# An encoder's opening: zero products ahead of x, sums turned by transposes, later mask additions, new priorities, residual products last

## The chip, the cores and the metric

The kernel runs on one core of one Trainium2 chip. The metric is the device time of one execution in microseconds (us); lower is better. An execution's time is its span, from the first to the last instruction, and about 2 us around it.

## The reference, cut to what matters

Two layers of an encoder trunk work on x, 256 tokens of 1024 channels in float32. Each layer has a mixer and a feed-forward part, both conditioned by a vector c:

```python
mod = silu(c) @ ada_w + ada_b                     # six vectors of 1024
sh_m, sc_m, g_m, sh_f, sc_f, g_f = split(mod, 6)
h = rms_norm(x, norm_mix_g) * (1 + sc_m) + sh_m
proj = h @ w_in                                   # 1024 -> 5024 columns
(qa, ka, va, cq, ckv, kr, qc, kc, vc, ga, gb, gc) = split(proj)
o_na  = neighborhood_attention(qa, ka, va, na_rpb)
q_b   = rms_norm(cq, g) @ mla_w_uq;  kv_b = rms_norm(ckv, g) @ mla_w_ukv
o_mla = attention(...);  o_gqa = attention(...)   # merged by sigmoid gates, then w_out
x = x + g_m * (merged @ w_out)
h = rms_norm(x, norm_ffn_g) * (1 + sc_f) + sh_f
x = x + g_f * ((silu(gate) * up) @ ffn_w_down)    # gate, up = split(h @ ffn_w_gate_up)
```

After the second layer there is a last rms_norm. Matrix products are wanted in float32 accuracy.

## The kernel before, in words

**Products in three parts.** Each operand of a large product is split into a rounded part and the residual that the rounding leaves (`split_to`: a copy by ScalarE, a subtraction by VectorE). A product is then hi·whi + hi·wlo + lo·whi, lines L268, L269 and L270. Weights go through TensorE's moving side, 512 columns at a time, activations (`hi`, `lo`, 128x128) through the stationary side. The weights are cut into 248 items of up to 256 rows by 512 columns, 124 a layer. `load_split` fetches an item (SyncE issues the DMA, L247) and splits it into `whi` (ScalarE, L187) and `wlo` (VectorE, L188). There are five buffers for raw weights and seven for split ones. Each item is used twice, for the token halves t = 0 and t = 1. From item 12 on the second use stands four items behind the first.

**Order.** A list scheduler orders each engine's instructions: of those that are ready by its own model of the time, it takes the one with the smallest priority number, which is the place in the program unless `tc.high_priority()` moves it ahead. The queues that it writes are then worked off in order by each engine, whatever the chip's own times are. Within `tc.manual_schedule(engines={PE})` TensorE keeps the order of the program. `later(k, f)` puts a piece of work k uses of items behind; `at(i, f)` puts one ahead of item i.

**Opening.** x is loaded, squared and summed (`sumsq`, L192), scaled (L202), and turned by 16 transposes (`transposed`, L209), which ScalarE copies out (L834). The first layer's shift and scale (2 of the 6 vectors) are made a quarter (256 channels) at a time. `first_loads(q)` fetches 2 MB of `ada_w` in eight DMAs of 256 KB (L846). `first_sums(q)` forms eight products of 512 columns with `scz`, c's columns padded with zeros to 32, in four column groups of the array (L861); ScalarE copies the bank out as `four` (L864). In `four` the partial sums stand on rows 0, 32, 64 and 96. `first_mod(q)` adds them by four products of `four` with a column of ones (L870), makes A and B (L874 to L877), and modulates two of the eight channel blocks into `hi` and `lo` (L882 to L887). Items 0 to 11 are ordered so that the three items of a round need only the blocks of quarter q = 0, 1, 2, 3. `first_sums(q)` stands ahead of items 1, 4 and 7 (q = 1, 2, 3), `first_mod(q)` ahead of items 2, 5 and 8. Items 12 to 15 are the columns of qc. Item 16 (`mla_w_uq`) and item 17 (`mla_w_ukv`) take `cT` as their activations, item 18 begins the gates.

**cT.** `post_g1` copies cq, ckv and kr out of the bank (L363), squares them (L366), adds EPS (L370), takes the power -0.5 on GpSimd (L108), and scales (L374, L376). Nine uses later its second half `b_` transposes the result (L383), splits it into the two parts of `cT` (`split_to`, out `s`, in `tp`) and turns kr (L391 to L395).

**Masks.** `na_bias` fetches the relative position bias (two DMAs for each t, L345) and adds the window's mask to it, four VectorE additions for each t (L349). The first user is the softmax of the neighbourhood attention (L568), whose scores (L560) are formed ahead of item 18. In the first layer `na_bias` stands ahead of item 12. A softmax's result `P` goes to TensorE for transposes (L608).

## Time and profile before

| | |
|---|---|
| Median of 3 runs | 822.37 us (821.83 to 822.97) |
| The profiled execution: its own time | 822.51 us |
| Its span | 820.4 us |
| TensorE busy with matmuls | 790.7 us, 96% of the span |
| VectorE busy | 598.8 us, 73% |
| ScalarE busy | 453.7 us, 55% |
| Mean granted TensorE clock | 0.991 of full speed |
| DMA | 187.20 MB, mean 228 GB/s |

A row of a timeline gives the start, the length, the engine, the line in the kernel, the operation, what it writes and reads, and in brackets how long the engine was idle before it and what ended that idle time. PE is TensorE's matmul side, PEld its weight load, DVE VectorE, ACT ScalarE, POOL GpSimd, SPq SyncE's DMA queue. Busy times of matmuls overlap, so the start of the next matmul says more than the end of one.

### The profile page before, as it was taken

The page shows a single profiled execution, that of the slowest core. Times are in us where ns is not written, and L with a number is a line of the kernel's source. Part 1 is how long each engine was busy: PE and PEld are TensorE (multiplying, and loading weights), DVE is VectorE, ACT ScalarE, POOL GpSimd, SP SyncE. Part 2 cuts the span into 40 slices and gives each one's busy share as a digit, 9 for nine tenths or more (in the row PEclk, how much of TensorE's full clock was granted, in tenths as well). Part 3 has the DMA queues.
Part 4 walks back from the last instruction along what each step waited for, and adds up shares of the span by engine and source line. Part 5 has one row for each costly group of instructions (what it writes and reads, how often), then busy time and mean ns, then how long its engine had stood idle before and what let it go on. Part 6 is the DMA issues. An engine that isn't in the chain of part 4 may idle for free.

```text
span 820.4 us, 10803 instructions
## 1 busy us (share of the span) xinstructions
PE 790.7 (96%) x3776; PEld 633.4 (77%) x3776; DVE 598.8 (73%) x955; ACT 453.7 (55%) x788; POOL 25.8 (3%) x40
## 2 busy tenths in 40 slices
PE   5998999999999999999999999999999999999996
PEld 3786776788878888888878877777887888888884
DVE  3369898789777888875667699878978666665462
ACT  4365887644485444443466687774448544444441
POOL 1002100000000000000000020000000000000000
PEclk9999999999999999999999999999999999999998
DMA  9979488697667989886874668778765677876631
GB/s 315 359 245 273 131 293 252 198 311 227 194 180 241 322 294 306 276 264 190 210 213 137 180 192 279 222 230 283 250 198 182 219 233 223 259 226 184 182 103 52
DMA packets 113414, 187.20 MB, mean 228 GB/s; under 512 B 14672, under 2 KB 34256, under 8 KB 113360
## 3 DMA queue, kind: packets, MB, share of 16 engines
q1 hardware_dynamic: 113360, 186.51, 73.1%
q8 instruction: 30, 0.49, 0.3%
q14 instruction: 24, 0.20, 0.1%
HBM read 185.44 MB, written 1.05 MB: 227 GB/s over the span
## 4 chain that ended last, share of the span: by engine, by line
issue 49%; PE 31%; DVE 8%; DMA 6%; ACT 4%; POOL 1%; POOLq 0%; DVEq 0%; ACTq 0%
PE mm L268 8%; PE mm L270 8%; PE mm L269 8%; DMA raw<-in_ada_w_dram 6%; DVE wlo L188 2%; DVE acc L140 2%; PE tp L861 1%; POOL sm L108 1%; PE o L629 1%; ACT P L587 1%; ACT tm L218 1%; DVE sm L574 1%; PE tp L209 1%; PE tp L608 1%; PE tp L560 1%
## 5 line engine op out<-in xcount | busy, mean ns | idle before, releaser
L188 DVE TENSOR_TENSOR wlo<-raw,whi 128x1024 fp32r<-128x1024 f32 (+2 forms) x248 | 298.3, 1209 | 115.0 <-ACT whi L187 114.8
L187 ACT CAST whi<-raw 128x1024 fp32r<-128x1024 f32 (+2 forms) x248 | 256.9, 1041 | 221.6 <-PE mm L270 137.1
L268 PE MATMUL mm<-whi,hi 128*128 128x512 f32 (+1 forms) x784 | 314.0, 400 | 1.8 <-ACT hi L882 1.1
L270 PE MATMUL mm<-whi,lo 128*128 128x512 f32 (+1 forms) x784 | 307.1, 392 | 0.2
L269 PE MATMUL mm<-wlo,hi 128*128 128x512 f32 (+1 forms) x784 | 306.1, 390 | 0.5 <-DVE wlo L188 0.4
L268 PEld LDWEIGHTS mm<-whi,hi 128*128 128x128 f32 x784 | 148.1, 189 | 34.7 <-issue 5.7
L270 PEld LDWEIGHTS mm<-whi,lo 128*128 128x128 f32 x784 | 147.7, 188 | 32.8 <-DVE lo L188 1.8
L269 PEld LDWEIGHTS mm<-wlo,hi 128*128 128x128 f32 x784 | 148.3, 189 | 28.9 <-DVE wlo L188 1.7
L140 DVE SCALAR_TENSOR_TENSOR acc<-raw,sc,acc 128x512 f32<-128x512 f32 x140 | 104.9, 749 | 32.2 <-DMA raw<-in_ada_w_dram 30.5
L270 PE MATMUL mm<-whi,s 128*128 128x512 f32 (+1 forms) x188 | 73.3, 390 | 2.4 <-DVE s L188 2.4
L268 PE MATMUL mm<-whi,s 128*128 128x512 f32 (+1 forms) x188 | 74.2, 395 | 0.4 <-ACT s L187 0.4
L269 PE MATMUL mm<-wlo,s 128*128 128x512 f32 (+1 forms) x188 | 73.1, 389 | 0.0
L270 PEld LDWEIGHTS mm<-whi,s 128*128 128x128 f32 x188 | 35.4, 189 | 9.8 <-DVE s L188 2.6
L268 PEld LDWEIGHTS mm<-whi,s 128*128 128x128 f32 x188 | 35.3, 188 | 7.9 <-ACT s L187 0.9
L269 PEld LDWEIGHTS mm<-wlo,s 128*128 128x128 f32 x188 | 35.4, 188 | 6.8
L592 ACT ACTIVATE P<-P,sm 128x256 f32<-128x256 f32 x64 | 29.3, 509 | 5.7 <-DVE sm L590 5.6
L587 ACT ACTIVATE P<-tp,sm,rq 128x256 f32<-128x256 f32 x32 | 17.8, 561 | 15.9 <-DVE sm L584 15.8
L197 POOL TENSOR_SCALAR sm<-ss 128x1 f32<-128x1 f32 x10 | 4.0, 404 | 662.4 <-ACT tm L192 662.4
L218 ACT ACTIVATE tm<-tp,cm,cm 128x128 f32<-128x128 f32 x48 | 21.3, 472 | 6.2 <-PE tp L209 6.2
L108 POOL TENSOR_TENSOR sm<-sm,nhalf 128x1 f32<-128x1 f32 (+2 forms) x22 | 18.4, 835 | 127.1 <-DVE sm L370 65.2
L192 ACT ACTIVATE tm<-x_sb 128x512 f32<-128x512 f32 x20 | 12.6, 632 | 16.8 <-DVE x_sb L703 14.6
L733 DVE TENSOR_TENSOR tm<-tm,mm 128x512 f32<-128x512 f32 (+1 forms) x24 | 15.4, 640 | 8.7 <-PE mm L270 7.1
(157 smaller groups left out, 637.7 us busy)
## 6 DMA issues: line engine op xcount, KB each, us to landing
raw<-in_ada_w_dram SPq DMA_DIRECT2D x80, 512.0 KB, 4.8
raw<-in_w_gu_dram SPq DMA_DIRECT2D x80, 512.0 KB, 4.6
raw<-in_w_in_dram SPq DMA_DIRECT2D x64, 512.0 KB, 4.6
raw<-in_w_dn_dram SPq DMA_DIRECT2D x44, 512.0 KB, 4.8
s<-in_ada_w_dram SPq DMA_DIRECT2D x32, 256.0 KB, 6.7
raw<-in_w_out_dram SPq DMA_DIRECT2D x16, 512.0 KB, 4.9
raw<-in_w_in_dram SPq DMA_DIRECT2D x16, 256.0 KB, 5.0
raw<-in_w_gqa_dram SPq DMA_DIRECT2D x8, 512.0 KB, 5.6
```

The lines of the kernel that those rows point to most:

```text
L108: nc.gpsimd.tensor_tensor(out=r, in0=ms, in1=nhalf[:, 0:n], op=ALU.pow)
L140: nc.vector.scalar_tensor_tensor(out=acc, in0=raw[:, j, :], scalar=sc[:, kc:kc + 1], in1=acc, op0=ALU.mult, op1=ALU.add)
L187: nc.scalar.copy(hi_ap, src)
L188: nc.vector.tensor_tensor(out=lo_ap, in0=src, in1=hi_ap.bitcast(F32), op=ALU.subtract)
L192: nc.scalar.activation(junk, x_sb[:, t, hf * 512:(hf + 1) * 512], AF.Square, scale=1.0 / 32.0, accum_out=ss[:, hf:hf + 1])
L218: nc.scalar.activation(fv[:, j, :], xT[:, j, :], AF.Identity, scale=A[:, kc:kc + 1], bias=B[:, kc:kc + 1])
L268: nc.tensor.matmul(ps[t][:, 0:n], lhs(t, 0, kc), hi[:, j, 0:n], start=first, stop=False)
L269: nc.tensor.matmul(ps[t][:, 0:n], lhs(t, 0, kc), lo[:, j, 0:n], start=False, stop=False)
L270: nc.tensor.matmul(ps[t][:, 0:n], lhs(t, 1, kc), hi[:, j, 0:n], start=False, stop=last)
L587: nc.scalar.activation(pt[:, t, :], src[:, t, :], AF.Exp, bias=nb[:, t:t + 1], scale=scale[t], accum_out=rs[:, t:t + 1])
L592: nc.scalar.activation(pt[:, t, :], pt[:, t, :], AF.Copy, scale=rc[:, t:t + 1])
L733: nc.vector.tensor_tensor(out=hd[:, 0:n], in0=sgv, in1=up, op=ALU.mult)
```

## The change

Six edits are made together.

1. Sixteen products of 128x512 zeros (`warm`) stand on TensorE ahead of x's transposes, one more after `first_sums(0)` and one after `first_mod(0)`; their sums are read by nothing. The opening up to there is put in program order on TensorE.
2. `first_mod` no longer multiplies `four` with ones: it transposes its four blocks, and VectorE adds the four columns 0, 32, 64, 96 of each (`tensor_reduce`).
3. What follows in `first_mod` is a function of its own, `first_apply`, with high priority.
4. The mask additions become `na_mask`, five items behind the DMAs in the first layer (ahead of item 17), at the same place in the second.
5. `post_g1`'s chain from EPS to the scaled vectors, and the split of `cT`, get high priority.
6. Within an item the order over its two row blocks becomes hi·whi, hi·whi, hi·wlo, hi·wlo, lo·whi, lo·whi.

`tc.issue_after(last_pe())` only keeps TensorE's part of items 0 to 11 behind what was traced before it.

```diff
--- before.py
+++ after.py
@@ -91,6 +91,8 @@
 
     ones = cpool.tile([P, 1], F32, name="ones")
     nc.vector.memset(ones, 1.0)
+    zero1 = cpool.tile([P, 1], F32, name="zero1")
+    nc.vector.memset(zero1, 0.0)
     ones1 = cpool.tile([P, 2], F32R, name="ones1")
     nc.vector.tensor_copy(ones1, ones.to_broadcast([P, 2]))
     onesr = ones1[:, 0:1].to_broadcast([P, P])
@@ -262,12 +264,12 @@
                 if u == 0:
                     ps[t] = bank(t) if bank else psmm.tile([P, 512], F32, tag="mm", name=nm("mm"))
                 hi, lo = it["w"]
-                for j in range(nk):
-                    kc = 2 * u + j
-                    first, last = kc == 0, kc == nkc - 1
-                    nc.tensor.matmul(ps[t][:, 0:n], lhs(t, 0, kc), hi[:, j, 0:n], start=first, stop=False)
-                    nc.tensor.matmul(ps[t][:, 0:n], lhs(t, 0, kc), lo[:, j, 0:n], start=False, stop=False)
-                    nc.tensor.matmul(ps[t][:, 0:n], lhs(t, 1, kc), hi[:, j, 0:n], start=False, stop=last)
+
+                for n_, (part, w) in enumerate(((0, hi), (0, lo), (1, hi))):
+                    for j in range(nk):
+                        kc = 2 * u + j
+                        nc.tensor.matmul(ps[t][:, 0:n], lhs(t, part, kc), w[:, j, 0:n], start=(kc == 0 and n_ == 0),
+                                         stop=(kc == nkc - 1 and n_ == 2))
 
             pf = None
             if u == nu - 1:
@@ -337,13 +339,18 @@
 
         def na_bias():
             st["bias"] = []
+            st["hk"] = []
             for t in range(NT):
                 hk = t4([P, 16, W])
                 for r in range(2):
                     base = rpb[l, 2 * t + r]
                     src = bass.AP(tensor=base.tensor, offset=base.offset, ap=[[1, W], [127, 16], [1, W]])
                     nc.sync.dma_start(hk[r * W:(r + 1) * W], src)
-                b = t4([P, 16, W])
+                st["hk"].append(hk)
+
+        def na_mask():
+            for t in range(NT):
+                hk, b = st["hk"][t], t4([P, 16, W])
                 rev = bass.AP(tensor=hk.tensor, offset=hk.offset + W - 1, ap=[list(hk.ap[0]), [W, 16], [-1, W]])
                 for h in range(4):
                     nc.vector.tensor_tensor(out=b[:, 4 * h:4 * h + 4, :], in0=rev[:, 4 * h:4 * h + 4, :],
@@ -367,14 +374,15 @@
             nc.scalar.activation(junk[:, 256:384], c[:, 256:384], AF.Square, scale=float(128.0 ** -0.5),
                                  accum_out=s[:, 1:2])
             ms = sm(2)
-            nc.vector.tensor_scalar_add(ms, s, EPS)
-            r = rstd_of(ms, 2)
             rw = st["rw"]
             cn = t2([P, 384])
-            nc.vector.scalar_tensor_tensor(out=cn[:, 0:256], in0=c[:, 0:256], scalar=r[:, 0:1], in1=rw[:, 0:256],
-                                           op0=ALU.mult, op1=ALU.mult)
-            nc.vector.scalar_tensor_tensor(out=cn[:, 256:384], in0=c[:, 256:384], scalar=r[:, 1:2], in1=rw[:, 256:384],
-                                           op0=ALU.mult, op1=ALU.mult)
+            with tc.high_priority():
+                nc.vector.tensor_scalar_add(ms, s, EPS)
+                r = rstd_of(ms, 2)
+                nc.vector.scalar_tensor_tensor(out=cn[:, 0:256], in0=c[:, 0:256], scalar=r[:, 0:1], in1=rw[:, 0:256],
+                                               op0=ALU.mult, op1=ALU.mult)
+                nc.vector.scalar_tensor_tensor(out=cn[:, 256:384], in0=c[:, 256:384], scalar=r[:, 1:2],
+                                               in1=rw[:, 256:384], op0=ALU.mult, op1=ALU.mult)
 
             def b_():
                 tpt = tpb()
@@ -383,7 +391,8 @@
                     nc.tensor.transpose(tv[:, j, :], cn[:, j * P:(j + 1) * P], ident)
                 cT = t4([P, 2, 3, P], F32R)
                 st.setdefault("cT", {})[t] = cT
-                split_to(cT[:, 0], cT[:, 1], tv[:, 0:3, :])
+                with tc.high_priority():
+                    split_to(cT[:, 0], cT[:, 1], tv[:, 0:3, :])
                 kr = c[:, 384:416]
                 kpe = st["kpe"][:, t, :]
                 ab = t2([P, 2, 32])
@@ -651,6 +660,7 @@
         flush.add(i0)
         at(i0 + (7 if l == 0 else 0), params)
         at(i0 + (12 if l == 0 else 8), na_bias)
+        at(i0 + (17 if l == 0 else 8), na_mask)
 
 
         st["m"] = {}
@@ -822,6 +832,18 @@
         layer(l)
     xT0 = {}
 
+    warm_w = ppl.tile([P, 512], F32R, tag="pp", name="warm_w")
+    nc.vector.tensor_copy(warm_w, zero1.to_broadcast([P, 512]))
+    warm_ps = pso.tile([P, 512], F32, tag="o", name="warm_ps")
+
+    def warm(n):
+
+        for _ in range(n):
+            nc.tensor.matmul(warm_ps, warm_w[:, 0:P], warm_w, start=True, stop=True)
+
+    def last_pe():
+        return next(i for i in reversed(nc.cur_bb.bb.instructions) if i.engine == mybir.EngineType.PE)
+
     def first_x():
         xT = act.tile([P, KC, S], F32, tag="lo", name=nm("xT"))
         for hf in range(2):
@@ -865,9 +887,15 @@
         return four
 
     def first_mod(q, four):
-        red = tpb()
+        pv = tpb().rearrange("p (j q) -> p j q", j=4)
         for j in range(4):
-            nc.tensor.matmul(red[:, j:j + 1], four[:, j * P:(j + 1) * P], ones, start=True, stop=True)
+            nc.tensor.transpose(pv[:, j, :], four[:, j * P:(j + 1) * P], ident)
+        red = sm(4)
+        nc.vector.tensor_reduce(out=red, in_=pv.rearrange("p j (r z) -> p j r z", z=32)[:, :, :, 0], op=ALU.add, axis=AX.X)
+        with tc.high_priority():
+            first_apply(q, red)
+
+    def first_apply(q, red):
         k0 = 2 * q
         A, B, hT = mods[(0, 1)], mods[(0, 0)], state[0]["hT"]
         r2 = sm(2)
@@ -905,8 +933,13 @@
                 step(1, pend.pop(0))
         if i == 0:
             raws = first_loads(0)
-            first_x()
-            first_mod(0, first_sums(0, raws))
+            with tc.manual_schedule(engines={mybir.EngineType.PE}):
+                warm(16)
+                first_x()
+                four = first_sums(0, raws)
+                warm(1)
+                first_mod(0, four)
+                warm(1)
         for f in side.get(i, ()):
             f()
         load_split(it)
@@ -915,7 +948,7 @@
             q1 = i // 3 + 1
             if i % 3 == 1 and q1 < 4:
                 raws = first_loads(q1)
-            with tc.manual_schedule(engines={mybir.EngineType.PE}):
+            with tc.issue_after(last_pe()), tc.manual_schedule(engines={mybir.EngineType.PE}):
                 if i % 3 == 1 and q1 < 4:
                     four = first_sums(q1, raws)
                 if i % 3 == 2 and q1 < 4:
```

## Rows read from the trace of the kernel before

**Rows 1.** Windows: busy us and count by engine, granted clock, DMA share.

```profile
core 0: us, PE busy (x) PEld busy (x) DVE busy (x) ACT busy (x) POOL busy (x), PEclk, DMA share, GB/s
...
13.40:16.80 3.40, 2.21 (x16) 1.14 (x12) 0.35 (x3) 1.37 (x2) 0.00 (x0) 1.00 1.07 368
16.80:20.20 3.40, 2.34 (x6) 1.83 (x7) 3.35 (x6) 2.03 (x3) 0.00 (x0) 0.50 1.10 349
...
78.20:81.60 3.40, 3.40 (x13) 2.50 (x11) 3.40 (x9) 1.39 (x4) 0.00 (x0) 0.51 0.52 131
...
125.00:800.00 675.00, 667.00 (x3162) 540.58 (x3161) 509.39 (x754) 372.07 (x623) 13.79 (x20) 1.00 0.73 226
```

**Rows 2.** Timeline of the opening, TensorE.

```profile
7.82 3.68 PE L209 MATMUL tp<-con,tm 128*128 128x128 f32 x16 [7.82 <-DVE tm L202]
...
15.30 1.05 PE L870 MATMUL tp<-ones,tm 128*128 128x1 f32 x8 [0.73 <-ACT tm L864]
...
17.49 0.72 PE L268 MATMUL mm<-whi,hi 128*128 128x416 f32 x1 [1.14 <-ACT hi L882]
...
24.98 0.50 PE L268 MATMUL mm<-whi,hi 128*128 128x512 f32 x1
...
25.55 0.39 PE L270 MATMUL mm<-whi,lo 128*128 128x512 f32 x1
...
25.78 0.40 PE L268 MATMUL mm<-whi,hi 128*128 128x512 f32 x1
...
26.01 0.39 PE L269 MATMUL mm<-wlo,hi 128*128 128x512 f32 x1
...
33.84 1.92 PE L861 MATMUL tp<-s,scz 128*32 128x512 f32 x16
35.69 0.50 PE L268 MATMUL mm<-whi,hi 128*128 128x512 f32 x1
...
46.41 0.50 PE L268 MATMUL mm<-whi,hi 128*128 128x512 f32 x1
```

**Rows 3.** Quarter q = 1, last DMA: issue, then KB and us to landing.

```profile
15.82 0.37 SPq L846 DMA_DIRECT2D s<-in_ada_w_dram  x1
...
s<-in_ada_w_dram SPq DMA_DIRECT2D x1, 256.0 KB, 6.0
```

**Rows 4.** The same for q = 3.

```profile
38.25 0.37 SPq L846 DMA_DIRECT2D s<-in_ada_w_dram  x1
...
s<-in_ada_w_dram SPq DMA_DIRECT2D x1, 256.0 KB, 5.5
```

**Rows 5.** Timeline of TensorE around item 16.

```profile
66.42 0.49 PE L383 MATMUL tp<-con,tm 128*128 128x128 f32 x3
...
73.23 0.44 PE L268 MATMUL mm<-whi,s 128*128 128x384 f32 x1 [0.44 <-ACT s L187]
...
74.11 0.66 PE L407 MATMUL tp<-con,tm 128*128 128x128 f32 x4 [0.25 <-ACT s L408]
77.14 0.44 PE L270 MATMUL mm<-whi,s 128*128 128x384 f32 x1 [2.38 <-DVE s L188]
```

**Rows 6.** Timelines of ScalarE and VectorE around item 16.

```profile
72.72 0.85 ACT L187 CAST s<-tp 128x384 fp32r<-128x384 f32 x2
...
75.20 1.42 DVE L349 TENSOR_TENSOR s<-s,con 128x256 f32<-128x256 f32 x4
76.54 1.01 DVE L188 TENSOR_TENSOR s<-tp,s 128x384 fp32r<-128x384 f32 x2
...
82.82 0.42 DVE L568 SCALAR_TENSOR_TENSOR P<-tp,s 128x256 f32<-128x256 f32 x1 [0.55 <-PE tp L560]
```

**Rows 7.** Windows of VectorE to item 23; timeline row of its wlo.

```profile
62.50:97.10 34.60, 33.42 (x90) 0.95 0.73 193
97.10:102.50 5.40, 2.79 (x7) 1.00 0.69 237
...
101.24 1.22 DVE L188 TENSOR_TENSOR wlo<-raw,whi 128x1024 fp32r<-128x1024 f32 x1
```

## Prediction

> **What bounds the kernel now.** I read the windows first. From 125 to 800 us TensorE is busy 667 of 675 us at the full clock [rows 1], so behind the opening the kernel is as long as TensorE's work, and what is saved ahead of that reaches the end unless a later wait takes it back. Then I looked for the places ahead of 125 us where TensorE is idle or granted half its clock (1.2 GHz, not 2.4). There are two.
>
> The first is the opening. Item 0 starts at 17.49 us [rows 2]. Behind the stretch 13.4 to 16.8, in which TensorE was busy 2.21 of 3.40 us, half the clock is granted [rows 1], and item 0 runs at that. But the DMA engines are full there (share 1.07 and 1.10) [rows 1]. Item 1 stands behind `first_sums(1)`, which needs a quarter's eight DMAs. The last of them is issued at 15.82 and lands 6.0 us later, at 21.8 [rows 3]; for q = 3 it is 38.25 and 5.5, so 43.75 [rows 4]. Items 1 and 7 start at 24.98 and 46.41 [rows 2]. The reader is to see how little lies between: 3.2 and 2.7 us.
>
> The second is item 16. TensorE waits 0.44 us for `cT`'s rounded part, 0.25 for a bank that ScalarE empties, and 2.38 for `cT`'s residual part [rows 5]. That subtraction stands on VectorE right behind four mask additions, which end at 76.6 [rows 6]; the idle stretch is followed by half the clock from 78.2 to 81.6 [rows 1].
>
> **The change part by part.** *Zero products.* At the full clock 512-column products start 0.23 us apart (25.55, 25.78, 26.01) [rows 2]; at half the clock an estimate is twice that. Sixteen cost 3.7 to 7.4 us. Their operands need a memset and one copy on VectorE, which feeds L209 only at 7.82 [rows 2], so an estimate is that they start at 2 us and end between 5.7 and 9.4. The transposes begin at 7.82 [rows 2], so they may be held 1.6 us. That costs nothing: the sums behind them end with a landing, not with TensorE. If it went the other way and the clock is full, the 16 transposes need half of 3.68 us [rows 2], and this too ends at the landing. The two single products lie in TensorE's waits of 0.73 and 1.14 us [rows 2].
>
> What the clock can give is therefore bounded by the landings. `first_sums` comes in four steps, 1.85 us in all (33.84 to 35.69) [rows 2]; two of them, 0.9 us, may lie behind the last landing. Item 1 can then start at 21.8 + 0.9 = 22.7 instead of 24.98, 2.3 us earlier. Item 7 can start at 43.75 + 0.9 = 44.65 instead of 46.41 [rows 2], 1.75 us earlier. As the DMAs ran full before and are not changed, the later landing counts: **−1.75**. The lower end: TensorE stays at half the clock, and item 1 is won only by the 0.4 of the new sums and the 0.46 of the order within item 0 (both below), 0.9 in all.
>
> *Transposes for sums.* Eight steps by ones take 1.05 us (L870) [rows 2]; four transposes take 0.66 (L407) [rows 5]. The added reduction is a small VectorE operation; from the rows I have it lies between nothing and the 0.42 us of an operation on 256 columns [rows 6]. So 0.4 us less against 0 to 0.4 more in a chain whose end the landings set: 0. For q = 1 to 3 TensorE saves 0.4 us each, which the landings take too, but for the last: within the range.
>
> *Residual products last.* The number of products and weight loads stays. Before, L269 follows L268 with the same stationary block; afterwards no neighbours share one. From L270 to L268, which need different blocks, it is 0.23 us, from L268 to L269, which share one, 0.23 as well [rows 2]: sharing brought nothing that the rows show, so losing it costs 0, and at most what two decimals hide. For lateness the edit moves the first need of `wlo` by one product (0.23 us) and of a residual by two (0.46): at item 16 it would shorten the one long wait by 0.46, which the next edit removes whole. I take 0.
>
> *Masks and priorities.* The split of `cT` moves ahead of what ScalarE and VectorE did first. Its last transposes begin at 66.42 [rows 5], six us before ScalarE gets to it at 72.72, without an idle time ahead [rows 6]: its place in the queue made it late. With priority it is early, and the waits of 0.44, 0.25 and 2.38 go: **−3.0**. Without the idle stretch the clock stays, and what ran from 78.2 to 81.6 at half the clock [rows 1] takes half as long: **−1.7**. The mask additions, eight in 2.8 us (four take 1.42 [rows 6]), are still due ahead of L568, and VectorE was idle for only 0.55 us there, waiting for the scores [rows 6].
>
> *Given back.* TensorE would be 1.75 + 3.0 + 1.7 = 6.45 us ahead. Its next need that VectorE sets is `wlo` of item 23, made from 101.24 to 102.5 [rows 7]; counted in items, that is when TensorE takes item 23 up. From 62.5 to 97.1 VectorE is busy 33.42 of 34.60 us and then 2.79 of 5.40 [rows 7]: 3.8 us idle. Its inputs come 1.75 us earlier. If it closes all its idle time, it is 5.55 us ahead, and 0.9 us is given back; if none, 4.7. Much of that idle time is waiting for work that TensorE sends, and the end with it closed is the nearer one; I take **+1.8**.
>
> The profiled execution took 822.51 us, its span of 820.4 and 2.1 around it, which nothing here touches. The sum is −1.75 −3.0 −1.7 +1.8 = −4.65, so 817.86 for it; the median of the runs, 822.37, lies 0.14 lower, which makes **817.7 us** of the forecast. The cases below are worked from 822.4.
>
> **Rivals.** *Nothing is given back but 0.9*, or less because the scheduler orders VectorE anew (work with time in hand, as `wlo` of items 19 to 22, moves behind the softmax): 822.4 − 6.45 + 0.4 = 816.3. For it speaks that VectorE's order was written for a late TensorE.
>
> *VectorE's backlog takes it all:* the 4.7 us come back at the softmax and item 23, and only the opening's 1.75 is left: 820.7. For it speaks VectorE's 33.42 of 34.60 us.
>
> *The clock falls in the opening as before.* Ahead of item 0 TensorE has transposes, sums that wait for landings, and single products, which is not more than the 2.21 of 3.40 us after which half the clock was granted [rows 1]. Item 0 then runs at half the clock, as it did; the start of item 1 is won only by 0.9, and one of the two rounds behind it adds the 0.4 of its new sums before the landings stop it: 1.3 instead of 1.75, so 818.2. The Trainium skill speaks for this rival ("TensorE: Matmul & The Clock Gate", Part 4: PE-mode transpose): it says that transposes do not count as work for the clock gate, and both the turned x and the new sums are transposes. The trace neither agrees nor disagrees: transposes stood ahead of the full clock of 13.4, but sums stood between.
>
> *The other side: the neighbourhood softmax becomes late, twice.* If VectorE does the masks and the `wlo` of later items ahead of L568, its first softmax can start no later than its work then allows, 82.82 − 1.75 = 81.1, while the scores are there 6.45 us earlier than before, at 76.4. TensorE stands at L608 until the result comes, up to 4.7 us; an idle stretch of 2.4 us was enough to lose the clock (1.7 more). Once gives 822.4 − 6.45 + 6.4 = 822.4, no change. It decides when the second pair of heads, whose softmax stands behind the first in the same queue, loses the clock a second time: 824.1. Against it: VectorE never has more to do than before.
>
> **How the numbers follow.** The forecast's own case has 0.5 (816.8 to 819.5), little given back 0.17, the clock's case 0.1, the backlog 0.16, the late softmax 0.07. Below 0.2% (1.65 us), which is about what a measurement of this kernel tells from no change, "faster" ends at 820.7: the first three cases and half the backlog, 0.85. "Same" has the other half of the backlog and some of the late softmax, 0.1; "slower" 0.05. The range leaves out the late softmax and the outer ends of the others: 815.2 to 820.9.
>
> **What would show it.** Item 1's first product (L268, 512 columns) near 22.7 and item 7's near 44.6, both right behind a landing; no wait of L270 for `s` near 72 us, with `cT`'s casts on ScalarE close behind L383; full clock from about 24 us on; the waits that are left near L568, L608 and item 23. The prediction is wrong if the landings themselves come earlier or later, if `cT`'s cast stays behind the casts of weights, or if the list scheduler, whose choices downstream I cannot read from this trace, moves a wait into the steady part.

## The result and the profile after

Four runs of the changed kernel gave a median of 816.57 us (816.25 to 816.87), four of the kernel before beside them 822.67 (821.83 to 824.28): a ratio of 0.9917 [0.9897, 0.9938], faster by more than the 0.2% from which the prediction counts a change. The forecast was 817.7, its range 815.2 to 820.9. The profiled execution took 816.62 us, its span 814.7. Of the terms of the forecast some were too large and some too small, and one gain was put down to the wrong edit; the experiments show which.

Three windows of the changed kernel, their columns as in [rows 1]; the last is that of item 0:

```profile
78.20:81.60 3.40, 3.40 (x19) 2.44 (x19) 2.42 (x4) 2.89 (x7) 0.00 (x0) 1.00 0.27 84
125.00:800.00 675.00, 666.65 (x3162) 541.35 (x3161) 506.00 (x749) 368.73 (x615) 13.79 (x20) 1.00 0.70 225
...
17.00:20.40 3.40, 2.52 (x10) 1.80 (x11) 3.34 (x6) 2.03 (x3) 0.00 (x0) 1.00 1.10 348
```

Look at the granted clock, the third number from the end: 1.00 in every one, where in the kernel before two stretches had half of it. TensorE's work behind 125 us is what it was (666.65 us against 667.00), so nearly all of the gain was made ahead of that.

TensorE's timeline of the opening, to lay beside [rows 2]:

```profile
1.44 5.32 PE L842 MATMUL warm_ps<-warm_w 128*128 128x512 f32 x16 [1.44 <-DVE warm_w L836]
...
20.98 2.51 PE L883 MATMUL tp<-s,scz 128*32 128x512 f32 x16
23.42 0.73 PE L271 MATMUL mm<-whi,hi 128*128 128x512 f32 x2
...
26.28 0.60 PE L892 MATMUL tp<-con,tm 128*128 128x128 f32 x4
26.64 0.70 PE L271 MATMUL o<-whi,hi 128*128 128x512 f32 x2
...
30.59 0.79 PE L271 MATMUL mm<-whi,lo 128*128 128x416 f32 x2 [0.21 <-DVE lo L915]
...
34.29 0.73 PE L271 MATMUL mm<-whi,hi 128*128 128x512 f32 x2
...
43.30 1.92 PE L883 MATMUL tp<-s,scz 128*32 128x512 f32 x16
45.16 0.73 PE L271 MATMUL mm<-whi,hi 128*128 128x512 f32 x2
```

Item 1 starts at 23.42 instead of 24.98, item 4 at 34.29 instead of 35.69, item 7 at 45.16 instead of 46.41. The first is bound by a landing, the last isn't. The last DMAs of q = 1 and q = 3, first when SyncE issues them, then KB and the time to landing, against [rows 3, 4]:

```profile
16.30 0.37 SPq L868 DMA_DIRECT2D s<-in_ada_w_dram  x1
...
37.86 0.37 SPq L868 DMA_DIRECT2D s<-in_ada_w_dram  x1
```

```profile
s<-in_ada_w_dram SPq DMA_DIRECT2D x1, 256.0 KB, 6.0
...
s<-in_ada_w_dram SPq DMA_DIRECT2D x1, 256.0 KB, 5.5
```

They land at 22.3 and 43.4. The sums ahead of item 1 take 2.51 us, stretched by the landing that falls into them. Those ahead of item 7 take 1.92, as long as sums that wait for nothing took before [rows 2]: TensorE got to them just as the last DMA landed.

VectorE in the first round behind item 1 shows why it wasn't there earlier:

```profile
26.92 0.17 DVE L894 TENSOR_REDUCE sm<-tp 128x4 f32<-128x16 f32 x1 [0.60 <-PE tp L892]
27.01 1.01 DVE L190 TENSOR_TENSOR wlo<-raw,whi 128x832 fp32r<-128x832 f32 x1
...
28.98 1.22 DVE L190 TENSOR_TENSOR wlo<-raw,whi 128x1024 fp32r<-128x1024 f32 x1
30.11 0.76 DVE L915 TENSOR_TENSOR lo<-tm,hi 128x256 fp32r<-128x256 f32 x2
```

The same two steps in the kernel before:

```profile
30.68 0.75 DVE L887 TENSOR_TENSOR lo<-tm,hi 128x256 fp32r<-128x256 f32 x2
31.35 1.22 DVE L188 TENSOR_TENSOR wlo<-raw,whi 128x1024 fp32r<-128x1024 f32 x1
```

The new reduction takes only 0.17 us, but with it VectorE's order is another: a `wlo` of 1.22 us now stands ahead of hT's residual `lo`, and not behind it. So `lo` comes too late for item 3 (TensorE's row at 30.59), and likewise in items 6 and 9. The `wlo` of 1.01 us isn't the difference: the kernel before has one of 1.02 us in the same chain, at 29.09.

Item 16 of the changed kernel: TensorE, then ScalarE, then VectorE, against [rows 5, 6].

```profile
65.34 0.49 PE L391 MATMUL tp<-con,tm 128*128 128x128 f32 x3
...
69.10 0.63 PE L416 MATMUL tp<-con,tm 128*128 128x128 f32 x4 [0.46 <-DVE s L190]
...
66.13 0.84 ACT L189 CAST s<-tp 128x384 fp32r<-128x384 f32 x2
...
68.40 1.01 DVE L190 TENSOR_TENSOR s<-tp,s 128x384 fp32r<-128x384 f32 x2
```

The casts of `cT` follow its transposes within a microsecond instead of 6.3. Three waits of 3.07 us in all have become one of 0.46.

Behind that, the prediction looked for VectorE's backlog. TensorE's waits of 0.2 us and more in the stretch from there to 231 us in the kernel before and 224 in the changed one, by what ended them (us in all, times, the longest), first of the kernel before, without the one of item 16, then of the changed one, whose first row is the 0.46 above:

```profile
PE tp L560 <- DVE PT L611: 0.5, 1, 0.5
PE tp L481 <- ACT PT L613: 0.4, 1, 0.4
PE tp L608 <- ACT P L587: 0.3, 1, 0.3
```

```profile
PE tp L416 <- DVE s L190: 0.5, 1, 0.5
PE tp L481 <- DVE tm L432: 0.2, 1, 0.2
```

No wait has come for L577, L617 or item 23, and two of the old ones are gone. The same scores further on, before and after, and the place where TensorE next loses time:

```profile
150.05 1.24 PE L560 MATMUL tp<-s,s 96*128 96x256 f32 x5
```

```profile
143.15 1.67 PE L569 MATMUL tp<-s,s 96*128 96x256 f32 x7
...
299.97 0.73 PE L271 MATMUL mm<-wlo,hi 128*128 128x512 f32 x2 [1.08 <-DVE wlo L190]
```

### The profile page after: what moved, and what is told of

Read it like the earlier page. It is cut to its first block, busy times and chain, and to the rows that moved or that the text cites. A ratio compares the mean times of both kernels' runs of the same rounds, so it can differ in the third digit from the quotient of the medians.

```text
span 814.7 us, 10812 instructions
## 1 busy us (share of the span) xinstructions
PE 791.9 (97%) x3778; PEld 630.9 (77%) x3778; DVE 599.2 (74%) x961; ACT 454.1 (56%) x788; POOL 24.6 (3%) x40
## 3 DMA queue, kind: packets, MB, share of 16 engines
HBM read 185.44 MB, written 1.05 MB: 229 GB/s over the span
## 4 chain that ended last, share of the span: by engine, by line
issue 49%; PE 31%; DVE 7%; ACT 6%; DMA 5%; POOL 1%; SPq 0%; POOLq 0%; DVEq 0%; ACTq 0%
PE mm L271 24%; DVE wlo L190 3%; DMA raw<-in_ada_w_dram 2%; PE tp L569 2%; DMA raw<-in_w_mla_dram 2%; DVE acc L142 1%; PE o L638 1%; ACT P L596 1%; PE tp L617 1%; ACT whi L189 1%; PE tp L883 1%; ACT tm L220 1%; DMA con<-in_consts_dram 1%; DMA s<-in_ada_w_dram 1%; ACT P L601 1%
## 5 line engine op out<-in xcount | busy, mean ns | idle before, releaser
L271 PE MATMUL mm<-whi,hi 128*128 128x512 f32 (+1 forms) x784 | 249.8, 399 | 1.9 <-ACT hi L910 1.1
L271 PE MATMUL mm<-wlo,hi 128*128 128x512 f32 (+1 forms) x784 | 242.9, 391 | 1.2 <-DVE wlo L190 1.1
L271 PE MATMUL mm<-whi,lo 128*128 128x512 f32 (+1 forms) x784 | 242.2, 390 | 0.6 <-DVE lo L915 0.6
L271 PEld LDWEIGHTS mm<-wlo,hi 128*128 128x128 f32 x784 | 146.5, 188 | 32.4 <-DVE wlo L190 2.3
L271 PEld LDWEIGHTS mm<-whi,hi 128*128 128x128 f32 x784 | 141.1, 188 | 34.0 <-issue 6.0
L271 PE MATMUL mm<-whi,s 128*128 128x512 f32 (+1 forms) x376 | 104.6, 390 | 0.0
L271 PE MATMUL mm<-wlo,s 128*128 128x512 f32 (+1 forms) x188 | 58.2, 388 | 0.0
L596 ACT ACTIVATE P<-tp,sm,rq 128x256 f32<-128x256 f32 x32 | 17.8, 563 | 12.5 <-DVE sm L593 12.5
L110 POOL TENSOR_TENSOR sm<-sm,nhalf 128x1 f32<-128x1 f32 (+2 forms) x22 | 18.4, 835 | 125.5 <-DVE sm L380 63.1
L194 ACT ACTIVATE tm<-x_sb 128x512 f32<-128x512 f32 x20 | 12.6, 632 | 16.8 <-DVE x_sb L713 14.6
L543 ACT ACTIVATE s<-mm 128x512 f32<-128x512 f32 x24 | 14.3, 595 | 9.9 <-PE mm L271 9.9
L617 PE MATMUL tp<-con,P 128*128 128x128 f32 x128 | 19.0, 276 | 0.3 <-DVE G L177 0.3
```

Source lines behind the costliest of these rows:

```text
L110: nc.gpsimd.tensor_tensor(out=r, in0=ms, in1=nhalf[:, 0:n], op=ALU.pow)
L271: nc.tensor.matmul(ps[t][:, 0:n], lhs(t, part, kc), w[:, j, 0:n], start=(kc == 0 and n_ == 0), stop=(kc == nkc - 1 and n_ == 2))
L543: nc.scalar.activation(st["gate"][gi][:, t, :], ps, AF.Tanh, scale=0.5)
L596: nc.scalar.activation(pt[:, t, :], src[:, t, :], AF.Exp, bias=nb[:, t:t + 1], scale=scale[t], accum_out=rs[:, t:t + 1])
L617: nc.tensor.transpose(tv[:, k, t * P:(t + 1) * P], pts[i][:, t, k * P:(k + 1) * P], ident)
```

## The experiments

Times are medians; each ratio is against runs of the kernel before on the same chip.

| Run | What differs | us (lowest to highest, runs) | Ratio |
|---|---|---|---|
| e1 | changed, no zero products | 816.46 (815.95 to 817.69, 4) | 0.9927 [0.9906, 0.9947] |
| e2 | changed, sums by ones | 815.71 (814.73 to 815.89, 4) | 0.9913 [0.9889, 0.9937] |
| e3 | changed, old order in an item | 818.06 (817.48 to 818.88, 4) | 0.9945 [0.9924, 0.9965] |
| e4 | changed, masks where they were | 818.07 (817.15 to 819.38, 4) | 0.9945 [0.9923, 0.9967] |
| e5 | changed, no priorities in `post_g1` | 815.37 (814.53 to 817.31, 4) | 0.9907 [0.9881, 0.9934] |
| e6 | before, residual products last | 821.95 (821.15 to 824.83, 10) | 0.9993 [0.9975, 1.0012] |
| e7 | changed, reduction with priority | 817.37 (817.07 to 817.92, 4) | 0.9929 [0.9906, 0.9952] |
| e8 | e2, `ada_w` loads ahead of the item's | 819.72 (817.75 to 822.65, 10) | 0.9964 [0.9946, 0.9983] |
| e9 | before, masks five items later | 816.34 (814.65 to 817.14, 4) | 0.9914 [0.9886, 0.9942] |
| e10 | e9 and e6 together | 816.27 (815.84 to 816.75, 4) | 0.9916 [0.9891, 0.9942] |
| e11 | e2 and e5 together | 815.13 (814.18 to 817.98, 5) | 0.9916 [0.9887, 0.9945] |
| e12 | changed, mask additions left out | 814.20 (813.10 to 814.91, 4) | 0.9890 [0.9863, 0.9916] |

The kernel before itself ran from 819.87 to 826.46 us over 19 executions beside e5 to e8, so medians that lie a microsecond apart are not told apart here; the traces are.

One thing has to be known of the opening before its traces are compared. Item 1 waits for the last DMA of quarter q = 1, and how long behind its landing it starts goes with the granted clock of that profiled execution (all in us):

| Profile | Half the clock | Last landing of q = 1 | Item 1 | `cT`'s first transposes | From item 1 to these |
|---|---|---|---|---|---|
| changed | not here | 22.3 | 23.42 | 63.62 | 40.20 |
| e2 | not here | 21.8 | 22.94 | 63.04 | 40.10 |
| e5 | 17.8 to 21.2 | 22.0 | 23.66 | 63.88 | 40.22 |
| e11 | 18.1 to 21.5 | 21.6 | 23.68 | 63.40 | 39.72 |
| e7 | 19.8 to 23.2 | 22.3 | 24.37 | 64.58 | 40.21 |
| e3 | 19.7 to 23.1 | 22.3 | 24.54 | 65.49 | 40.95 |
| e6 | 19.0 to 22.4 | 21.9 | 24.08 | 63.80 | 39.72 |
| e10 | 18.4 to 21.8 | 21.7 | 23.90 | 63.66 | 39.76 |
| before | 16.8 to 23.6 | 21.8 | 24.98 | 64.70 | 39.72 |
| e9 | 18.2 to 25.0 | 22.1 | 25.81 | 65.54 | 39.73 |

Item 1 starts 1.1 us behind the landing at the full clock, 1.7 to 2.3 us behind it with 3.4 us of half the clock, and 3.1 to 3.7 us with 6.8 us. What an edit does to the rounds themselves stands in the last column: 39.7 us with sums by ones in either order, 40.2 with transposes, 41.0 with transposes in the old order. (In e2's 40.10 are 0.4 us by which its sums ahead of item 4 are stretched by a landing.)

**e1, no zero products.**

```diff
-                warm(16)
                 first_x()
                 four = first_sums(0, raws)
-                warm(1)
                 first_mod(0, four)
-                warm(1)
```

> The changed kernel without its 18 products of zeros and their operands; all else kept. Theory (the zeros keep the clock full in the opening, and the start of item 1 is bounded by landings): half the clock is granted behind about 16.8 us again, item 0 runs at it, item 1 starts near 24.1 instead of 23.4 and the whole takes 0.5 to 1.0 us longer than the changed kernel's 816.6. Rival 1 (landings alone set the opening): item 1 within 0.2 us of 23.4, no change. Rival 2 (the zeros are worth everything that the opening won): 1.2 us or more longer.

816.46 against 816.57: the eighteen products bring nothing that can be measured. Half the clock was granted in e1 from 19.4 to 22.7 us. Item 1 starts at 23.71, 2.0 us behind a landing at 21.7: the clock cost 0.9 us there, and the earlier landing gave 0.6 back. The end is the same.

**e2, sums by products with ones again.**

```diff
-        pv = tpb().rearrange("p (j q) -> p j q", j=4)
+        red = tpb()
         for j in range(4):
-            nc.tensor.transpose(pv[:, j, :], four[:, j * P:(j + 1) * P], ident)
-        red = sm(4)
-        nc.vector.tensor_reduce(out=red, in_=pv..., op=ALU.add, axis=AX.X)
+            nc.tensor.matmul(red[:, j:j + 1], four[:, j * P:(j + 1) * P], ones, start=True, stop=True)
```

> The changed kernel with the sums formed by products with ones again, as before, first_apply's priority kept. Theory (each round's transposes save 0.45 us of TensorE, but the longer chain makes the residual part late, 0.6 us at item 3, 6 and 9): rounds get shorter by 0.0 to 0.2 us each, the whole is the same or up to 0.6 us faster than 816.6. Rival (the transposes pay as they look on TensorE): 3 x 0.45 = 1.3 us slower.

815.71. The list of TensorE's waits from 18 to 64 us is empty in e2's trace, and the first transposes of `cT` stand at 63.04 us, where the changed kernel has them at 63.62. But 0.48 of this 0.58 stands already at item 1, because the landing came 0.5 us earlier (the table). What the transposes cost is read from e11 beside e5, which differ in the sums alone and start item 1 at the same time: 39.72 us against 40.22 from there, so 0.5 us in three rounds. Each set of transposes saves TensorE 0.45 (0.36 to the next product against 0.81), and item 3 loses 0.63 (its products take 2.97 us, from 29.46 to the sums at 32.43; in e2 2.34). The end doesn't show it: at 143 us e2 and the changed kernel are level (143.23 and 143.15).

**e3, the old order in an item.**

```diff
-                for n_, (part, w) in enumerate(((0, hi), (0, lo), (1, hi))):
-                    for j in range(nk):
-                        kc = 2 * u + j
-...
+                for j in range(nk):
+                    kc = 2 * u + j
+                    (hi·whi, hi·wlo, lo·whi of this j)
```

> The changed kernel with the old order within an item (hi by whi, hi by wlo, lo by whi for each row block). Theory (the order only postpones waits for wlo and the residual part): TensorE's waits in the opening rounds grow by 0.2 to 0.45 us each at items 0, 3, 6 and 9, so 0.8 to 1.6 us slower than 816.6; the pace of products, 0.23 us apart, stays. Rival (the order costs or saves pace everywhere): a difference that grows along the kernel, 2 us or more either way.

818.06; e2, on the same chip but with sums by ones besides, took 815.71 and has no run in common with it. TensorE's waits in e3 from 18 to 66 us:

```profile
PE mm L272 <- DVE lo L915: 1.7, 3, 0.6
...
PE mm L271 <- DVE wlo L190: 0.6, 1, 0.6
```

1.7 us of waits for `lo` instead of the changed kernel's 0.6, and 0.6 more for item 0's `wlo`. By the table the rounds behind item 1 take 0.7 us longer for it (40.95 against 40.20). Item 1 itself starts 1.1 us later than the changed kernel's, but e7, which has the changed kernel's order and half the clock at the same place, is 0.95 later too. So 0.7 us are shown to be the order's; the rest of the 1.5 between the medians isn't placed.

**e4, the masks where they were, the priorities kept.**

```diff
-        at(i0 + (17 if l == 0 else 8), na_mask)
+        at(i0 + (12 if l == 0 else 8), na_mask)
```

> The changed kernel with the mask additions again right behind their DMAs, ahead of item 12; the priorities kept. Theory (the priority alone takes the split of cT out of the late place): no wait of TensorE over 0.6 us near item 16, within 0.5 us of 816.6. Rival (the masks were what the residual part of cT waited for): a wait of 1 to 2.4 us returns and perhaps half the clock with it, 818 to 821.

818.07, and the long wait is back. TensorE, ScalarE and VectorE of e4, and then the window behind:

```profile
74.93 0.63 PE L416 MATMUL tp<-con,tm 128*128 128x128 f32 x4 [2.51 <-DVE s L190]
...
68.52 1.05 ACT L189 CAST whi<-raw 128x1024 fp32r<-128x1024 f32 x1
...
70.00 0.85 ACT L189 CAST s<-tp 128x384 fp32r<-128x384 f32 x2
...
73.57 0.75 DVE L356 TENSOR_TENSOR s<-s,con 128x256 f32<-128x256 f32 x2
74.24 1.01 DVE L190 TENSOR_TENSOR s<-tp,s 128x384 fp32r<-128x384 f32 x2
```

```profile
76.40:79.70 3.30, 3.30 (x12) 2.43 (x11) 3.30 (x9) 2.87 (x6) 0.00 (x0) 0.50 0.25 48
```

Even with priority the cast stands behind a cast of weights, and the subtraction behind mask additions. The half clock is back too. Yet e4 is 4.2 us faster than the kernel before beside it (822.22), so the other five edits make a gain without this one. `cT`'s first transposes come 0.75 us earlier, the wait is 2.51 instead of 3.07, and the scores at 146.62 us are 3.4 us ahead of the kernel before; which of the five gives how much of this wasn't tried.

**e5, the masks later, no priority in `post_g1`.**

```diff
-            with tc.high_priority():
-                nc.vector.tensor_scalar_add(ms, s, EPS)
-...
+            nc.vector.tensor_scalar_add(ms, s, EPS)
+...
-                with tc.high_priority():
-                    split_to(cT[:, 0], cT[:, 1], tv[:, 0:3, :])
+                split_to(cT[:, 0], cT[:, 1], tv[:, 0:3, :])
```

> The changed kernel with the priorities of `cn` and of the split of `cT` taken away; the masks still come five items later. The prediction credits the priority with taking the 3.07 us of waits at item 16 away, and calls the masks only not yet due. By that theory the split of `cT` falls back behind the casts and splits of the weights that ScalarE and VectorE have in their queues: `cT`'s cast near 70 us or later, a wait of L416 for `s` of 1 us or more, and 817.5 to 819 us. The rival, which the run with the masks moved back supports: it is the place of the masks alone, since without them nothing of any length stands ahead of the subtraction; then the wait stays below 0.7 us and the time is 816 to 817. Between them: 1 us of wait, part each.

815.37, and the wait is what it is with the priority:

```profile
69.37 0.63 PE L414 MATMUL tp<-con,tm 128*128 128x128 f32 x4 [0.49 <-DVE s L190]
```

With e4 this settles that pair: the place of the masks takes the long wait away, the priority does nothing that a run shows.

**e6, the kernel before with the residual products last.** (The loop of e3's minus lines, put into the kernel before.)

> The kernel before with one edit of the change: the residual products last in each weight item. The prediction takes 0 for it, and at most 0.46 us where a wait for `s` ends an idle stretch, so 821.8 to 822.4 us. The rival comes from the run with the old order, which was 1.5 us slower than the changed kernel: what is made late by DVE (the residuals of weights and of hT) is needed up to four products later, in every item of the opening, so items 3, 6 and 9 and item 16 wait less; 820 to 821.2 us, with the wait of L270 for `s` at 2.0 us or less and item 7 starting 0.5 us or more before 46.41.

821.95, ratio 0.9993: nothing. Item 7 starts 0.9 us earlier, as the rival had it, but not for its reason: the rounds behind item 1 take what they took (39.72 us). The 0.9 us lie ahead of item 1, where a wait of 0.37 for item 0's `wlo` is gone and half the clock lasted 3.4 us instead of 6.8; whether the order shortened that isn't shown. So `cT`'s first transposes come earlier too (63.80 instead of 64.70), but the wait behind them grows from 3.07 to 4.9 us:

```profile
74.80 0.62 PE L269 MATMUL mm<-whi,s 128*128 128x384 f32 x2 [2.87 <-ACT s L187]
...
78.48 1.01 PE L269 MATMUL mm<-whi,s 128*128 128x384 f32 x2 [1.80 <-DVE s L188]
...
73.32 1.04 ACT L187 CAST whi<-raw 128x1024 fp32r<-128x1024 f32 x1 [0.97 <-DMA raw<-in_w_in_dram]
74.28 0.85 ACT L187 CAST s<-tp 128x384 fp32r<-128x384 f32 x2
```

Between the first two lies one of 0.25, as before. The last two rows are ScalarE's: the cast of `cT` stands behind a cast of weights that it has to wait for, so coming earlier doesn't help.

**e7, the reduction inside the stretch of high priority.**

```diff
-        nc.vector.tensor_reduce(out=red, in_=pv..., op=ALU.add, axis=AX.X)
         with tc.high_priority():
+            nc.vector.tensor_reduce(out=red, in_=pv..., op=ALU.add, axis=AX.X)
             first_apply(q, red)
```

> The changed kernel with the added reduction inside the stretch of high priority, beside `first_apply`. Theory: items 3, 6 and 9 wait 0.6 us each for hT's residual because VectorE makes a `wlo` of 1.01 us between the reduction and `first_apply`'s first step; the reduction is late or early as the planner sees it, and with it in the stretch the two stand together. Then the three waits fall to 0.1 us or less, items 4 and 7 start 0.5 and 1.0 us earlier (33.8 and 44.2 us), and the end comes 0.5 to 1.5 us earlier: 815 to 816. Rival: the `wlo` stands there because the planner holds `first_apply` for another input, so the order and the waits stay: 816.5, as the changed kernel. A third case: item 7 comes earlier, and the later waits at the softmax take it back: 816.3 or more.

The rival held in the order and the waits. The scheduler (the planner of the expectations) leaves both `wlo` where they were, that of 1.01 us behind the reduction, at 27.95, and the one that delays `lo`, which the theory overlooked:

```profile
29.92 1.22 DVE L190 TENSOR_TENSOR wlo<-raw,whi 128x1024 fp32r<-128x1024 f32 x1
31.06 0.76 DVE L916 TENSOR_TENSOR lo<-tm,hi 128x256 fp32r<-128x256 f32 x2
```

The three waits for `lo` are 0.6 us in all, as without the edit. Why the scheduler sets the `wlo` there was not found.

**e8, `ada_w`'s loads ahead of the item's own, with e2's sums.**

```diff
+        q1 = i // 3 + 1
+        if i < 12 and i % 3 == 1 and q1 < 4:
+            raws = first_loads(q1)
         load_split(it)
         if i < 12:
-            q1 = i // 3 + 1
-            if i % 3 == 1 and q1 < 4:
-                raws = first_loads(q1)
```

> The changed kernel with the sums by products with ones again, and with each quarter's loads issued ahead of the weight item's own loads instead of behind them. The first alone gave 815.7. Theory of the prediction for item 1: its start is set by the landing of q = 1, so it comes as much earlier as the landing does, 0.5 to 0.9 us (to 22.5 to 22.9), while items 4 and 7 come earlier only by what item 1 gave, since TensorE sets them; the end 815.0 to 815.5 if it is kept. Rival: the loads that are moved back (weights of items 5, 8, 11) land later and their items wait, or the softmax takes the gain back: 815.7 or more.

819.72, slower than its sibling e2. The last DMA of q = 1 lands 1.0 us earlier (20.8), and item 1 still starts later:

```profile
24.62 0.73 PE L271 MATMUL mm<-whi,hi 128*128 128x512 f32 x2 [1.68 <-ACT whi L189]
```

Item 7 waits 1.65 in the same way. What is moved ahead in a full queue moves something else back: here the weights of items 1 and 7 themselves.

**e9, the kernel before with the masks five items later.**

```diff
+                st["hk"].append(hk)
+
+        def na_mask():
+            for t in range(NT):
+                hk, b = st["hk"][t], t4([P, 16, W])
...
         at(i0 + (12 if l == 0 else 8), na_bias)
+        at(i0 + (17 if l == 0 else 8), na_mask)
```

> The kernel before with one edit of the change: the mask additions come five items later; no priority, the old order in an item, the old opening. If the place of the masks alone makes the split of `cT` late, the waits for `s` at item 16 fall from 3.07 us to below 1 us, the half clock behind them goes, and what the softmax gives back is left over: 818 to 819.5 us (the changed kernel with the old order gave 818.1). By the prediction's words, that the priority brings the split forward, the wait stays near 3 us, and the time is 822.

816.34: this one edit gives all of the change's gain that the runs can tell, more than either theory expected. TensorE's wait for `s` and ScalarE's cast in e9:

```profile
70.31 0.63 PE L412 MATMUL tp<-con,tm 128*128 128x128 f32 x4 [0.76 <-DVE s L188]
...
68.05 0.84 ACT L187 CAST s<-tp 128x384 fp32r<-128x384 f32 x2
```

The edit adds and takes away nothing on ScalarE, but the scheduler's order for it changes. In the kernel before a copy that waited 2.11 us for VectorE and two casts of weights stood ahead of `cT`'s cast at 72.72 [rows 6]:

```profile
69.41 0.59 ACT L456 COPY tm<-mm 128x512 f32<-128x512 f32 x1 [2.11 <-DVE tm L393]
...
70.83 1.99 ACT L187 CAST whi<-raw 128x1024 fp32r<-128x1024 f32 x2
```

The edit also takes the buffers of the masked bias later from the pool that `cT`'s buffer comes from. Whether the additions themselves or these buffers set the order, no run shows.

e9's opening had half the clock for 6.8 us, as the kernel before, and its span is the changed kernel's: 814.7. But it didn't win it in the same place. The scores, which the changed kernel begins 6.9 us ahead of the kernel before, e9 begins 4.4 us ahead:

```profile
145.62 1.89 PE L565 MATMUL tp<-s,s 96*128 96x256 f32 x8
```

That alone is what its theory had expected (818 to 819.5). The other 1.3 us come in the second layer, around 540 us, most of them from two waits there; first the kernel before, then e9, in which only the first is left:

```profile
PE o L629 <- DVE PT L611: 0.8, 1, 0.8
PE tp L608 <- DVE G L175: 0.7, 1, 0.7
```

```profile
PE o L634 <- DVE PT L616: 0.4, 1, 0.4
```

The changed kernel has 0.8 and 0.3 there. That the two end level is a sum of different gains.

**e10, masks later and residual products last, nothing else.** (The edits of e6 and e9.)

> The kernel before with two edits: masks five items later and the residual products last; nothing of the opening (no zero products, sums by products with ones, TensorE's order left to the planner) and no priority. Theory from the runs so far: these two make the whole gain, 815.4 to 816.7. Rival, the prediction's terms: the opening has its own share of 1.1 to 1.75 us that these two lack, 817.5 to 818.5. If the time is at the first, the gain in the opening before 64 us must be 0.7 us or more by the order alone.

816.27: the whole gain without any edit of the opening and without a priority. Its second transposes of `cT` stand at 65.38 us, the changed kernel's at 65.34. That isn't the order's doing alone, as the theory had it: its rounds take what they took before (39.76 us), and half the clock lasted 3.4 us where e9 and the kernel before had 6.8.

**e11, sums by ones and no priorities.** (The edits of e2 and e5.)

> The changed kernel with sums by products with ones again and without the priorities. Each alone gave 815.7 and 815.4. Theory: the sums' 0.6 us in the opening adds to a kernel that needs no priority: 814.5 to 815.4. Rival: what is won ahead of 64 us is taken back at the softmax, whose start VectorE sets, and it stays at 815.4 to 816.5.

815.13, within the theory's range, but its five runs reach from 814.18 to 817.98 and its ratio is the changed kernel's. No version here is faster than the change by more than its interval.

**e12, no mask additions.**

```diff
-                for h in range(4):
-                    nc.vector.tensor_tensor(out=b[...], in0=rev[...], in1=mask..., op=ALU.add)
-                st["bias"].append(b)
+                st["bias"].append(hk)
```

> The changed kernel without the eight mask additions: the softmax adds the bias rows as they were loaded, not masked and not turned, so this part of the computation is left out. Theory: the changed kernel is 7.6 us ahead at the scores (74 us) and 3.5 at 92 us because VectorE is late with the softmax; with 2.8 us (eight of 0.355) taken off VectorE ahead of the softmax, 2 to 3 us of that are not given back: 813.5 to 815 us. Rival: the softmax is late for another reason (ScalarE's exponentials, or work of VectorE that the planner puts there instead), and the time stays at 815.8 to 816.9.

814.20, in the theory's range for another reason. If VectorE's additions made the softmax late, e12 would be ahead behind it; it isn't. The scores that the changed kernel begins at 143.15 us begin here at:

```profile
143.24 1.03 PE L566 MATMUL tp<-s,s 96*128 96x256 f32 x4
```

So in the first layer the additions cost nothing where they now stand. Its span is 2.8 us shorter than the changed kernel's, and all of it is gained behind that. The wait of 1.08 us at 299.97 isn't there; but e1 to e5, which keep the additions, have no wait there either, so that isn't the additions' price. Of the waits of the second layer, that of 0.8 us for `PT` is gone. What this part owes to the additions wasn't tried.

## Why the prediction was right, and where it was not

Where the time went, from the two traces, against the terms:

| Term | Predicted | Trace | From |
|---|---|---|---|
| Opening, up to `cT`'s second transposes | -1.75 | -1.08 | 66.42 [rows 5] and 65.34 |
| Waits at item 16 | -3.0 | -2.61 | 3.07 [rows 5] and 0.46 |
| Half clock behind them | -1.7 | -1.7 | half of the 3.4 us of [rows 1]; full after |
| Short waits to 150 us | none | -1.0 | 1.2 and 0.2, the lists of waits |
| Given back | +1.8 at item 23 | about +1.2, the most of it at 300 us | 150.05 - 143.15 = 6.90, and 820.4 - 814.7 = 5.7 at the end |
| Sum | -4.65 | -5.7 | spans |

The first four make 6.4 of the 6.9 us by which TensorE is ahead at 143 us; the other 0.5 are in waits below 0.2 us or not placed. That the sum came within 1.05 us of the trace is in part luck: errors of up to 1.5 us stand on both sides of it.

*The waits at item 16 and the clock behind them* were sized rightly. The step that failed is the credit: "With priority it is early, and the waits of 0.44, 0.25 and 2.38 go", with the masks merely "still due ahead of L568". The priority without the masks' new place leaves 2.51 us and half the clock (e4); the masks alone leave 0.76 us and the full clock there (e9). The prediction read from [rows 6] that four additions stood right ahead of the subtraction, but didn't follow it back to the cast, where a waiting copy and two casts of weights stood ahead: the scheduler's order for ScalarE hung on where the additions were too. Nor did it see that the edits overlap: the masks alone give 6.3 us (e9), the other five without them 4.2 (e4), all six 6.1.

*The opening.* "The later landing counts" held for item 1, which starts 1.1 us behind a landing that came at 22.3, not 21.8. The prediction put 0.9 us behind it. The 1.56 us won at item 1 are the clock's, 1.1 us behind the landing instead of 3.1, less 0.5 for the later landing. Item 7 no landing binds: two rounds of TensorE's own work and the waits for `lo` set it. From item 1 to item 4 is 10.87 us, where it was 10.71 [rows 2]. And what is won there can't be told from the time: e9, whose opening was 0.84 us longer than that of the kernel before, ends level by gains further on.

*Transposes for sums: 0.* Mis-sized by 0.5 us (e11 beside e5). The reduction was inside its bounds (0.17 of 0 to 0.42); what was missed is the order that came with it, a `wlo` of 1.22 us ahead of `lo` on VectorE.

*Residual products last: 0.* Right by itself (e6: 0.9993; e10 against e9: 816.27 and 816.34), wrong beside the transposes, whose late `lo` it covers: without it the rounds lose 0.7 us (e3). The prediction counted one place where it shortens a wait, item 16; there were three more, items 3, 6 and 9. Sharing a stationary block brought nothing, as said: the rounds take 39.72 us in either order.

*Given back: +1.8.* VectorE's backlog at item 23 didn't appear, nor at the softmax: TensorE's waits of 69 to 224 us are 0.5 and 0.2. The rival "little given back" (816.3) came nearest in size; its reason, that the scheduler orders VectorE anew, was not tried by itself. About 1.2 came back far behind, most of it at a `wlo` at 300 us. That belongs to this execution: in e1 VectorE works in the same order there without a wait of TensorE, only the DMA that it waits for landed earlier (it goes on at 295.37 us, in the changed kernel at 296.84). The opening was too large by 0.7 and item 16 by 0.4; the give-back was too dear by 0.6, and 1.0 to 1.5 us of gain stood in no term. Together they make the 1.05 by which the sum was off.

*The clock's rival.* In the changed kernel's profiled execution the clock stayed full through the opening, from 4.4 us on. But zero products don't settle it: e5 has the same opening, and in its profiled execution half was granted during item 0:

```profile
17.90:21.20 3.30, 3.30 (x9) 2.88 (x10) 2.34 (x4) 0.88 (x1) 0.00 (x0) 0.50 1.11 349
```

Of the profiled executions with the zeros (the changed kernel, e2 to e5, e7, e8, e11, e12) three held the full clock through the opening and six lost it for a part; without them (the kernel before, e1, e6, e9, e10) all five lost it. The price at item 1 is 0.6 to 1.2 us for 3.4 us of half the clock (the table in the experiments). How much of it is left at `cT`'s first transposes goes with the landing and with how late the half clock ends: they stand at 64.58 in e7 and at 63.88 in e5, with the same waits in the rounds, against 63.62 us. At the end it can't be told: e1 and e9 lost the clock and are as fast.

The rule behind this rival (the Trainium skill, "TensorE: Matmul & The Clock Gate", Part 4: PE-mode transpose) says that transposes do not count as work for the gate. With the zeros and transposed sums one execution of six held the clock; with the zeros and sums by ones (e2, e8, e11) two of three did. That leans to the rule, on too few executions to show it.

## What to carry to other kernels

When a scheduler writes the queues, a late operation is late on each engine that it passes through: follow it back to the first queue in which something stands ahead of it, and look for the work whose place set that order, not only for what ended the wait. Take a change of several edits apart by adding each to the kernel before as well as by taking each away: here one edit alone made the whole gain and the other five, without it, two thirds of it; and the order of products was worth 0.7 us taken away and nothing added, because it paid for another edit. Before a difference in an opening is put down to an edit, read the granted clock and the landings of both traces. And a lead ahead need not be the lead at the end: e9 was 2.5 us behind the changed kernel at 143 us and ended level with it.

## What the runs showed of the hardware

The sixteen zero products took 5.32 us in the changed kernel's profiled execution and 6.77 us in e5's, the same instructions from the same 1.44 us on: they start 0.43 us apart until 4.2 us and 0.23 us apart from 4.5 us on in the one, and 0.43 us apart until 7.6 us in the other. How soon the full clock comes differs from one execution to the next. So does the time: e5's four took 814.53, 814.63, 816.11 and 817.31 us at mean granted clocks of 0.998, 0.998, 0.996 and 0.994. Eight DMAs of 256 KB put ahead of an item's own in SyncE's queue, at a DMA share of 1.1, made that item wait 1.7 us (e8).
